# Where the low half of each weight is made: engine chosen by time to use, retention split four units ahead, down units on both sets of banks

## Chip, cores and metric

The kernel runs on one core of a Trainium2 chip. The metric is the device time of one execution in microseconds (us); the time of a kernel is the median of its runs.

## What is computed

One step of a decoder of two layers on 576 tokens (512 of a prompt, 64 of 8 samples), all in fp32. In each layer:

```python
rq, rk, rv, rg, sq, sk, sv, mq, g_ret, g_swa, g_mem = split(x @ w_in)
ret_b = (silu(rg) * group_norm(retention(rq, rk, rv, state))) @ w_br_ret
swa_b = sink_window_attend(rope(sq), rope(sk), sv, cache) @ w_br_swa
mem_b = mem_attend(mq, memory_keys, memory_values) @ w_br_mem
merged = sigmoid(g_ret) * ret_b + sigmoid(g_swa) * swa_b + sigmoid(g_mem) * mem_b
x = layer_norm(ALPHA * x + merged @ w_out)
x = layer_norm(ALPHA * x + square(relu(x @ w_up)) @ w_down)
```

For the prompt the memory keys and values are computed from 256 memory tokens (`mem_prompt @ w_mem_kv`); for the samples they come from a cache, 2 MB of keys and 2 MB of values a layer and group of four samples.

## The kernel before

**Weights.** The weights are cut into units of 128x8x128 fp32 numbers (512 KB), 154 a layer, used one after the other. To keep fp32 accuracy a unit is used as two tiles: `hi`, its value rounded to fp32r, and `lo`, what is left. A unit's matmuls go by eight slots, and each slot has three (hi by x's high part, lo by x's high part, hi by x's low part), for each of two groups of tokens, A and B, 288 columns each: 24 matmuls a unit and group. So the low part is wanted one matmul after the high part. Unit names: `mk`, `mv` (memory keys and values), `rk`, `rq`, `rv`, `rg` (retention), `sk`, `sv`, `sq` (window), `mq`; `gr`/`br`, `gs`/`bs`, `gm`/`bm` (gate and branch), `wo` (output), `up`, `ua`/`ub`, `dh`, `dn` (MLP). The MLP's middle works on pairs `ua`/`ub` in seven half-size products (`pair_steps`, `block`: their sums and casts are on VectorE and ScalarE), and between the pairs stand the half units `dh` of the down projection.

**Making the low part** (`split`, L546). A unit is loaded by SyncE's queue (`fetch`). By the first route, the DMA route, ScalarE casts (hi), ScalarE writes minus hi into lo, and a DMA issued on GpSimd's queue adds the raw unit to it. By the second (`split_into`), hi is cast on ScalarE or VectorE, whichever the planner holds free sooner (`soonest`), and VectorE subtracts. Before, the DMA route is taken by every unit from the ninth on but the second units of `dh`.

**Order.** Everything is emitted in one order, and each engine's queue keeps it. `run` goes through the steps of a stage; between the matmuls of a step `Filler` puts other work (norms, attention, retention, and `tick`, which splits the next unit) by a planner's clock (`Clock`), whose cost of each instruction is in `cost` (L320 to L329), and by each unit's due time `use`: a split is emitted when the due time is within `LOOK` = 24 us, and at most `cap` units (three) stand split and unused; within `LEAD` = 4 us it is emitted at once. Of matmul results three PSUM banks (tag "g") take the units' products, and five (tag "a") the rest. 38 buffers of 4 KB a partition (tag "T") hold raw, hi and lo tiles and the cached memory; a tile's write waits until its buffer's last reader is done. `mem_sample` loads the cached memory on GpSimd's queue: two key tiles ahead, each other tile when the one two before it has been emitted to the matmuls.

**Names.** `load_mem` loads and prepares the memory tokens of layer 1 during layer 0's `dn`; `last` of `norm_ev` is the end of a group's layer norm, which is emitted in the next stage. Names of tiles are numbered as they are made; in the rows below `T` stands for any tile of the 38.

Of the kernel before, what the change touches and what calls it, by code (L numbers as in the profile page):

```python
# [36 lines left out]
EARLY = 0.4  # L37
EARLY_PE = -0.8
LEAD = 4.0
DN_SKEW = 7  # L40
START = 3
STEP = 2
# [178 lines left out]
def mm_us(n):  # L221
    return n / 2400.0 + 0.0134
# [40 lines left out]
def dn_skew(l):  # L263
    return 8 if l == DEPTH - 1 else DN_SKEW


class Clock:
# [41 lines left out]
    @staticmethod  # L309
    def cost(eng, fn, out, ins, kw):  # L310
        n = max([out.free_size()] + [i.free_size() for i in ins])
        if eng == "tensor":
            if fn == "transpose":
                return ins[0].partition_size() / 1200.0
            n, m = out.free_size(), out.partition_size()
            if ins[0].dtype == F32R:
                return mm_us(n if n >= 256 else 4 * n)
            return 4 * n / 2400.0 * (m / 128.0 if m < 128 else 1.0)
        psum = any(i.space == PSUM for i in ins)
        if eng == "scalar":  # L320
            t = (0.05 if psum else 0.094) + n / 1200.0
            return t + 0.093 * sum(kw.get(k) is not None and not isinstance(kw[k], float)
                                   for k in ("scale", "bias", "accum_out"))
        if eng == "gpsimd":
            return 0.15 + n / 480.0
        if fn == "bn_stats" or psum or len(ins) > 1 and fn != "tensor_scalar" or fn in ("tensor_reduce", "stream_shuffle"):
            return 0.068 + n / 960.0
        return 0.065 + 0.065 * (len(ins) - 1) + n / 1920.0

    def op(self, eng, fn, out, ins, kw, store):  # L330
        te = self.te
# [117 lines left out]
class Builder:  # L449
# [96 lines left out]
    def split(self, i):  # L546
        u, k, b = self.items[i]
        if b is not None:
            self.w[i] = self.block(u, b)
            self.live[i] = 1  # L550
            return
        raw = self.raw.pop(u)
        hi = self.tile([P, 8, P], F32R)
        lo = self.tile([P, 8, P], F32R)
        if u > 7 and (k[1] != "dh" or k[2] == 0):
            self.nc.scalar.copy(hi, raw)
            self.nc.scalar.activation(lo, raw, AF.Copy, scale=-1.0)
            self.nc.gpsimd.dma_start(lo, raw, accum_op=ALU.add)
        else:
            self.split_into(hi, lo, raw, True)  # L560
        self.w[i] = (hi, lo)
        self.live[i] = 2
# [25 lines left out]
    def tick(self):  # L588
# [6 lines left out]
        u = self.items[i][0]  # L595
        urgent = self.use[i] < self.fill.t + LEAD
        if urgent or c.te["scalar"] < c.now + 0.3 and (u not in self.raw or c.ready((self.raw[u],)) < c.now):
# [36 lines left out]
            if i % 2 and i < n - 1:  # L634
                self.fill.advance(6 * mm_us(cols))

    def mstep(self, u, g, X, evac, slots=range(8)):
        n = NG[g]

        def fn():  # L640
            ps = self.bank("g")[:, :n]
            self.gemm(ps, u, list(slots), lambda i: (X[g]["h"][i // 4][:, i % 4, :], X[g]["l"][i // 4][:, i % 4, :]))
            evac(g, ps)
        return ([u], fn, 6 * mm_us(n))

    def both(self, u, X, evac, slots=range(8)):
        return [self.mstep(u, g, X, evac, slots) for g in "AB"]

    def pair_steps(self, key, XT, evac):

# [83 lines left out]
    def load_x(self, X):  # L734
# [16 lines left out]
        def split():  # L751
            for i in range(4):
# [9 lines left out]
                X[g]["l"].append(lo)  # L762
        self.between = iter(todo)
        return split()

    def load_mem(self, M):
        M["h"] = [self.tile([P, 4, 256], F32R) for _ in range(2)]
        M["l"] = [self.tile([P, 4, 256], F32R) for _ in range(2)]
        raws = [self.tile([P, 4, 256]) for _ in range(2)]
        for j in range(2):  # L770
            self.nc.scalar.dma_start(raws[j], self.I["memT"][:, 4 * j:4 * j + 4, :])
        for j in range(2):
            yield (raws[j],)
            self.split_into(M["h"][j], M["l"][j], raws[j])

    def start(self):
        M = self.M = {}
        mem = [self.tile([P, 4, 256]) for _ in range(2)]
        M["h"] = [self.tile([P, 4, 256], F32R) for _ in range(2)]
        M["l"] = [self.tile([P, 4, 256], F32R) for _ in range(2)]  # L780
# [689 lines left out]
    def layer(self, l, X):  # L1470
# [2 lines left out]
        ident = self.c("ident")  # L1473
        uid = {k: self.item[(l,) + k, None] for k in unit_order() if k[0] not in ("ua", "ub")}
        M = self.M
        mk = self.tile([P, 4, 256])
        mv = self.tile([P, 2, 512])
        mkd = self.dram([P, 4, 256])
# [3 lines left out]
        steps = []  # L1482
# [64 lines left out]
        for p in range(4):  # L1547
# [8 lines left out]
            steps = []  # L1556
# [6 lines left out]
            if p == 0 and l:  # L1563
                steps = [steps[i] for i in (0, 2, 1, 3)]
            if p == 0:
                steps = [self.lazy(s, self.before[g]) for s, g in zip(steps, "AABB" if l else "ABAB")]
# [36 lines left out]
            def rg_ev(e, sg=sg):  # L1603
                def ev(g, ps):
                    t = self.tt()[:, :NG[g]]
                    S.activation(t, ps, AF.Tanh, scale=0.5)
                    V.scalar_tensor_tensor(sg[:, e, OFF[g]:OFF[g] + NG[g]], t, 1.0, ps, ALU.add, ALU.mult)
                return ev
            for e in range(2):
                steps += self.both(uid["rg", 2 * p + e], X, rg_ev(e))  # L1610
            self.run(steps)
            self.fill.add(self.retention(l, p, qk, rv, rvs, sg, GR), 3)

        del xs
        steps = []
# [72 lines left out]
        steps = []  # L1688
# [16 lines left out]
        mq = self.pair_tiles()  # L1705
        steps = []
# [30 lines left out]
        steps = []  # L1737
# [16 lines left out]
        steps = []  # L1754
# [46 lines left out]
        steps = []  # L1801
# [8 lines left out]
        def dh(q, k, src):  # L1810
            def ev(m):
                def e(g, ps):
                    if q == 0:
                        while len(Ts) <= (m % 4) // 2 and not self.fill.idle(tg):
                            self.fill.push(tg)
                        yt = y[g][m // 4][:, m % 4, :]
                        V.scalar_tensor_tensor(yt, yt, ALPHA, ps, ALU.mult, ALU.add)
                    else:
                        yt = y[g][m // 4][:, m % 4, :]
                        V.tensor_tensor(yt, yt, ps, ALU.add)  # L1820
                return e
            r = []
            for e in range(2):
                r += self.both(uid["dh", q, k], src, ev(2 * k + e), range(4 * e, 4 * e + 4))
            return r
        self.fill.add(tg, 2)
        steps = []
# [15 lines left out]
        for q in range(2, 8):  # L1843
            H.append(self.feat_tiles(1))
            steps = []
# [10 lines left out]
            if 2 < q < 5:  # L1856
                k = ("swk", "swv")[q - 3]
# [3 lines left out]
        if True:  # L1861
            keys = [("dn", m) for m in range(8)]
            n2 = {g: self.norm_ev(g, y[g], l, 16, EPS, X2) for g in "AB"}
            if X2 is not None:
                self.M = {}
                self.fill.add(self.load_mem(self.M), 5)
            self.run(skewed(keys, H, lambda m: lambda g, ps: n2[g](m, ps), dn_skew(l), "AB" if X2 else "BA"),
                     7 if X2 else 8)
            self.before = {g: lambda g=g: n2[g].st["last"] for g in "AB"}
# [84 lines left out]
```

## Time and profile before

| | us |
|---|---|
| median of three runs | 2315.34 (2314.46 to 2324.88) |
| the profiled execution | 2317.91 |
| its span, first to last instruction | 2316.1 |
| TensorE busy | 2161.7 |
| VectorE busy | 1176.4 |
| ScalarE busy | 1023.6 |
| GpSimd busy | 236.2 |

PE is TensorE, DVE VectorE, ACT ScalarE, POOL GpSimd, SP SyncE, PEld the loading of weights into TensorE. A row of waits says which engine stood, for what, how long in total, how often, and the longest. A row of a stretch gives from:to, its length, and for each engine the busy time with the number of instructions, then the TensorE clock that was granted (1.00 is 2.4 GHz, and the half of it, 1.2 GHz, is the other level), the share of the DMA engines and GB/s. A row by form gives busy time, the mean in ns of one, and the idle time before with what ended it. A row of the timeline gives start, length, engine, operation and, in brackets, the idle time before it and what ended it. Matmuls overlap, so busy time and idle time can add up to a little more than the stretch.

### The profile page before, as it was taken

Reading aid. Unit: us, or ns where it says so; the run is one execution under the profiler, and the core shown is the slowest. Engines: PE = TensorE matmul, PEld = TensorE weight load, DVE = VectorE, ACT = ScalarE, POOL = GpSimd, SP = SyncE. Lnnn points to the kernel's source line nnn. Section 1 sums busy time; section 2 is a strip of 40 time slices with the busy share of each in tenths; the row PEclk is TensorE's granted clock in tenths of the full one; section 3 lists DMA queues with packets and bytes.
Section 4 is the critical chain, followed back from the end, with each engine's and each line's share of the span. In section 5 each row is a group of like instructions: output and inputs, shape, how many; then the busy total and the mean of one; then the engine's idle time right before and its main releaser. Section 6 shows DMA issues by size and latency. Waiting matters only on the chain. (4 is left out here: it accounts for less than half of the span.)

```text
span 2316.1 us, 39366 instructions
## 1 busy us (share of the span) xinstructions
PE 2161.7 (93%) x16180; PEld 2082.1 (90%) x16180; DVE 1176.4 (51%) x2656; ACT 1023.6 (44%) x1853; POOL 236.2 (10%) x310
## 2 busy tenths in 40 slices
PE   7999999999988999997969999999989889999987
PEld 6999999988988999997969999999889879999987
DVE  4454554134237566665734446542332465666657
ACT  4333455434456443345443333554334554443453
POOL 1111201111111000000121111011111100000000
PEclk8999999999999999998979999999999989999999
DMA  9555645667585422235684557456776744222342
GB/s 321 133 134 134 171 113 147 162 183 198 147 219 114 123 86 73 84 100 145 174 213 125 140 144 181 113 137 164 190 202 158 186 107 115 94 73 81 100 121 69
DMA packets 97269, 328.63 MB, mean 142 GB/s; under 512 B 10624, under 2 KB 20352, under 8 KB 97024
## 3 DMA queue, kind: packets, MB, share of 16 engines
q0 software_dynamic: 41056, 149.97, 30.7%
q1 hardware_dynamic: 50944, 168.27, 21.2%
q10 hardware_dynamic: 5088, 7.87, 1.1%
q8 instruction: 127, 2.08, 0.4%
q14 instruction: 54, 0.44, 0.1%
HBM read 200.89 MB, written 15.99 MB: 94 GB/s over the span
## 5 line engine op out<-in xcount | busy, mean ns | idle before, releaser
L358 PE MATMUL pg<-T,T 128*128 128x288 f32 (+1 forms) x12992 | 1816.5, 299 | 116.0 <-DMA T<-T 85.3
L358 PEld LDWEIGHTS pg<-T,T 128*128 128x128 f32 x12992 | 1763.9, 191 | 154.8 <-DMA T<-T 92.6
L358 ACT CAST T<-T 128x1024 fp32r<-128x1024 f32 (+7 forms) x502 | 391.5, 801 | 222.2 <-DVE T L358 178.7
L358 POOL DMA_DIRECT2D T<-T x212 | 183.5, 870 | 1856.5 <-ACT T L358 1574.7
L358 PE MATMUL pa<-T,T 128*128 128x288 f32 (+9 forms) x2216 | 288.9, 314 | 22.5 <-DMA T<-in_mck 11.1
L358 DVE TENSOR_TENSOR T<-T,T 128x512 fp32r<-128x512 f32 (+5 forms) x351 | 273.0, 799 | 62.8 <-ACT T L358 59.2
L358 PEld LDWEIGHTS pa<-T,T 128*128 128x128 f32 (+3 forms) x2216 | 240.0, 170 | 48.4 <-issue 22.2
L358 ACT ACTIVATE T<-T 128x1024 fp32r<-128x1024 f32 (+1 forms) x224 | 237.7, 1062 | 27.2 <-DMA T<-T 11.7
L358 ACT ACTIVATE t<-pg 128x288 f32<-128x288 f32 x128 | 52.4, 409 | 229.8 <-PE pg L358 218.3
L358 DVE TENSOR_TENSOR T<-T,pg 128x288 f32<-128x288 f32 x208 | 90.5, 451 | 100.0 <-PE pg L358 99.5
L358 DVE TENSOR_TENSOR T<-u,T 128x288 fp32r<-128x288 f32 x160 | 72.8, 455 | 122.0 <-ACT T L358 121.9
L358 ACT ACTIVATE u<-u 128x288 f32<-128x288 f32 x200 | 88.8, 444 | 90.3 <-DVE u L358 86.2
L358 DVE SCALAR_TENSOR_TENSOR T<-t,pg 128x288 f32<-128x288 f32 x64 | 29.0, 454 | 141.6 <-ACT t L358 96.8
L358 ACT CAST T<-u 128x288 fp32r<-128x288 f32 x160 | 69.2, 433 | 52.0 <-DVE u L358 47.2
L358 DVE TENSOR_TENSOR T<-T,u 128x288 f32<-128x288 f32 (+2 forms) x136 | 88.1, 660 | 3.6
L358 DVE SCALAR_TENSOR_TENSOR u<-t,pg 128x288 f32<-128x288 f32 x64 | 28.8, 451 | 101.0 <-PE pg L358 100.7
L358 ACT COPY T<-pg 128x512 f32<-128x512 f32 (+2 forms) x44 | 20.9, 478 | 121.1 <-PE pg L358 120.9
L358 ACT ACTIVATE T<-pa,rnb,rr 128x128 f32<-128x128 f32 x32 | 12.0, 456 | 118.7 <-issue 86.9
L358 DVE TENSOR_TENSOR T<-pa,T 128x512 fp32r<-128x512 f32 (+2 forms) x48 | 25.3, 535 | 64.6 <-ACT T L358 64.1
L358 DVE TENSOR_TENSOR u<-u,pa 128x288 f32<-128x288 f32 x72 | 32.7, 454 | 45.2 <-PE pa L358 45.0
L358 ACT CAST T<-pa 128x256 fp32r<-128x256 f32 (+2 forms) x36 | 15.1, 419 | 60.6 <-PE pa L358 56.4
L358 PE MATMUL pa<-cst,T 128*128 128x128 f32 (+1 forms) x306 | 40.4, 276 | 0.0
(156 smaller groups left out, 1048.9 us busy)
## 6 DMA issues: line engine op xcount, KB each, us to landing
T<-in_wall SPq DMA_DIRECT2D x305, 512.0 KB, 4.2
T<-T POOLq DMA_DIRECT2D x212, 512.0 KB, 5.5
T<-in_mck POOLq DMA_DIRECT2D x16, 512.0 KB, 6.4
T<-in_mcv POOLq DMA_DIRECT2D x16, 512.0 KB, 6.7
T<-in_s POOLq DMA_DIRECT2D x8, 512.0 KB, 8.0
out_state_s<-T POOLq DMA_DIRECT2D x8, 512.0 KB, 5.5
T<-in_xT SPq DMA_DIRECT2D x4, 576.0 KB, 10.5
T<-in_xT ACTq DMA_DIRECT2D x4, 576.0 KB, 8.0
```

What stands on the lines that cost most here:

```text
L358: r = f(*a, **kw)
```

## The change

- `split` takes the DMA route only where the due time is more than `FAR` = 11 us from the planner's time, the unit isn't of `mq`, `gs`, `bs`, `gm`, `bm`, and stands behind the sixteenth. All others go to VectorE's subtraction. Of 212 units that took the DMA route 115 keep it and 97 leave it, 70 of them with the cast on ScalarE and 27 with the cast on VectorE; in 22 second units of `dh` the cast goes from VectorE to ScalarE.
- The planner's costs of ScalarE and VectorE instructions are higher, by 0.085 to 0.11 us each.
- `run` of retention may hold four units split, not three.
- The products of `dh` for group B go to the banks "a"; group A's stay in "g".
- At the start of layer 1 all of the memory tokens' preparation that is left is emitted before anything else.

```diff
+FAR = 11.0
...
         if eng == "scalar":
-            t = (0.05 if psum else 0.094) + n / 1200.0
+            t = (0.16 if psum else 0.19) + n / 1200.0
...
         if fn == "bn_stats" or psum or len(ins) > 1 and fn != "tensor_scalar" or fn in ("tensor_reduce", "stream_shuffle"):
-            return 0.068 + n / 960.0
-        return 0.065 + 0.065 * (len(ins) - 1) + n / 1920.0
+            return 0.155 + n / 960.0
+        return 0.15 + 0.065 * (len(ins) - 1) + n / 1920.0
...
-        if u > 7 and (k[1] != "dh" or k[2] == 0):
+        if self.use[i] - self.fill.t > FAR and k[1] not in ("mq", "gs", "bs", "gm", "bm") and u > 15:
             self.nc.scalar.copy(hi, raw)
             self.nc.scalar.activation(lo, raw, AF.Copy, scale=-1.0)
             self.nc.gpsimd.dma_start(lo, raw, accum_op=ALU.add)
...
-    def mstep(self, u, g, X, evac, slots=range(8)):
+    def mstep(self, u, g, X, evac, slots=range(8), tag="g"):
...
-            ps = self.bank("g")[:, :n]
+            ps = self.bank(tag)[:, :n]
...
-    def both(self, u, X, evac, slots=range(8)):
-        return [self.mstep(u, g, X, evac, slots) for g in "AB"]
+    def both(self, u, X, evac, slots=range(8), tags="gg"):
+        return [self.mstep(u, g, X, evac, slots, tag) for g, tag in zip("AB", tags)]
...
+        if l:
+            self.fill.finish(self.memory)
...
-            self.run(steps)
+            self.run(steps, 4)
             self.fill.add(self.retention(l, p, qk, rv, rvs, sg, GR), 3)
...
-                r += self.both(uid["dh", q, k], src, ev(2 * k + e), range(4 * e, 4 * e + 4))
+                r += self.both(uid["dh", q, k], src, ev(2 * k + e), range(4 * e, 4 * e + 4), "ga")
...
-                self.fill.add(self.load_mem(self.M), 5)
+                self.memory = self.load_mem(self.M)
+                self.fill.add(self.memory, 5)
```

Three places in the order of instructions. The first is VectorE between a pair and the `dh` units behind it, before: T923 and T925 collect the down projection of groups A and B, `pg` is a bank of "g".

```order
L358 TENSOR_TENSOR T923_6639<-T923_6639,pg1281_9292 128x288
L358 TENSOR_TENSOR T1229_8895<-u1280_9287,T1228_8894 128x288
L358 CAST T1284_9317<-T1251_9059 128x1024
L358 TENSOR_TENSOR T1285_9318<-T1251_9059,T1284_9317 128x1024
L358 TENSOR_TENSOR T925_6643<-T925_6643,pg1282_9307 128x288
L358 TENSOR_TENSOR T1288_9332<-T1271_9201,T1288_9332 128x512
L358 TENSOR_TENSOR T1290_9342<-T1271_9201,T1283_9315 128x1024
L358 TENSOR_TENSOR rc1291_9343<-T1290_9342,T1271_9201 128x512
L358 TENSOR_TENSOR T1292_9346<-rc1291_9343,T1292_9346 128x512
L358 TENSOR_TENSOR T923_6639<-T923_6639,pg1289_9335 128x288
L358 TENSOR_TENSOR T925_6643<-T925_6643,pg1293_9356 128x288
```

The same place after the change.

```order
L359 TENSOR_TENSOR T923_6604<-T923_6604,pg1281_9248 128x288
L359 TENSOR_TENSOR T1227_8849<-u1279_9224,T1226_8848 128x288
L359 TENSOR_TENSOR T925_6608<-T925_6608,pa1282_9263 128x288
L359 TENSOR_TENSOR T1229_8851<-u1280_9242,T1228_8850 128x288
L359 TENSOR_TENSOR T1285_9281<-T1252_9022,T1284_9280 128x1024
L359 TENSOR_TENSOR T1289_9295<-T1273_9172,T1289_9295 128x512
L359 TENSOR_TENSOR T923_6604<-T923_6604,pg1286_9284 128x288
L359 TENSOR_TENSOR T1290_9305<-T1273_9172,T1283_9278 128x1024
L359 TENSOR_TENSOR rc1291_9306<-T1290_9305,T1273_9172 128x512
L359 TENSOR_TENSOR T1292_9309<-rc1291_9306,T1292_9309 128x512
L359 TENSOR_TENSOR T925_6608<-T925_6608,pa1293_9312 128x288
```

Group B's products are read from `pa`, the 128x1024 cast has left VectorE, and one of the reads of `pg` stands ahead of the pair's sums (128x1024, then 128x512) where it stood behind them.

The second place is GpSimd's queue while the samples' first group reads its cached memory (`in_mck` keys, `in_mcv` values), before: each `T<-T` row is the low part of a unit.

```order
L358 DMA T690_5027<-in_mck 128x1024
L358 DMA T691_5029<-in_mck 128x1024
L358 DMA T706_5107<-T674_4923 128x1024
L358 DMA T718_5200<-T686_5011 128x1024
L358 DMA T725_5272<-in_mck 128x1024
L358 DMA T726_5278<-in_mck 128x1024
L358 DMA T729_5283<-T704_5104 128x1024
L358 DMA T733_5318<-in_mcv 128x1024
L358 DMA T734_5320<-in_mcv 128x1024
L358 DMA T748_5386<-T716_5197 128x1024
L358 DMA T750_5417<-in_mcv 128x1024
L358 DMA T752_5435<-in_mcv 128x1024
```

After the change.

```order
L359 DMA T690_5010<-in_mck 128x1024
L359 DMA T691_5012<-in_mck 128x1024
L359 DMA T740_5336<-in_mck 128x1024
L359 DMA T741_5342<-in_mck 128x1024
L359 DMA T742_5352<-in_mcv 128x1024
L359 DMA T743_5354<-in_mcv 128x1024
L359 DMA T757_5456<-in_mcv 128x1024
L359 DMA T758_5466<-in_mcv 128x1024
```

The low parts have left the queue, and the eight loads follow each other. Which buffer a load takes has changed with it: by the waits in front of the instructions, T740's load waits for the last matmul on T690 (the first key tile), T741's for the last on T691, and T758's for the last on T742 (the first value tile).

The third place is VectorE at the memory projection of layer 1, after the change: T1691, T1694 and T1697 are the low parts of `mv` 1 to 3, the other rows are group B's layer norm (T925, T926).

```order
L359 SCALAR_TENSOR_TENSOR u1679_12056<-pa1667_11963,ln1678_12054 128x288
L359 TENSOR_TENSOR T925_6608<-T925_6608,pa1666_11962 128x1152
L359 TENSOR_TENSOR ln1682_12082<-ln1681_12059 128x288
L359 SCALAR_TENSOR_TENSOR ln1682_12082<-ln1682_12082,u1679_12056 128x288
L359 SCALAR_TENSOR_TENSOR u1680_12057<-ln1682_12082,ln1681_12059 128x288
L359 TENSOR_TENSOR T925_6608<-T925_6608,u1680_12057 128x576 x2
L359 TENSOR_TENSOR T926_6609<-T926_6609,pa1666_11962 128x1152
L359 TENSOR_TENSOR T926_6609<-T926_6609,u1680_12057 128x576 x2
L359 TENSOR_TENSOR T1691_12106<-T1663_11950,T1690_12105 128x1024
L359 TENSOR_TENSOR T1694_12118<-T1671_11988,T1693_12117 128x1024
```

Before, the three are made by ScalarE and GpSimd, and GpSimd's queue has them in a row.

```order
L358 DMA d30_157<-T925_6643 128x4x288
L358 DMA d30_157<-T926_6644 128x4x288
L358 DMA T1691_12178<-T1669_12062 128x1024
L358 DMA T1694_12191<-T1679_12112 128x1024
L358 DMA T1697_12204<-T1689_12175 128x1024
```

On VectorE they now stand behind the norm, with twelve more of its instructions (128x288 and 128x576) between T1694 and T1697.

## Rows read from the trace of the kernel before

**Rows 1.** The page, busy time of each engine, share of the span, instructions.
```profile
PE 2161.7 (93%) x16180; PEld 2082.1 (90%) x16180; DVE 1176.4 (51%) x2656; ACT 1023.6 (44%) x1853; POOL 236.2 (10%) x310
```

**Rows 2.** Waits of PE over the whole span: total us, times, longest.
```profile
PE pg L358 <- DMA T<-T: 85.3, 27, 8.8
PE pg L358 <- DVE T L358: 25.2, 29, 1.4
PE pa L358 <- DMA T<-in_mck: 11.1, 4, 3.9
PE pa L358 <- DMA T<-in_mcv: 10.7, 10, 2.5
```

**Rows 3.** Waits of PE in 30:60, in 75:250, in 800:1060, in 1155:1190.
```profile
PE pg L358 <- DMA T<-T: 11.8, 2, 6.5
...
PE pg L358 <- DMA T<-T: 3.4, 4, 1.4
...
PE pg L358 <- DVE T L358: 10.1, 10, 1.0
...
PE pg L358 <- DMA T<-T: 18.9, 3, 8.6
```

**Rows 4.** Stretches: length; busy (count) of PE, PEld, DVE, ACT, POOL; clock; DMA.
```profile
34.00:42.00 8.00, 5.30 (x24) 5.29 (x25) 0.00 (x0) 2.58 (x4) 1.09 (x2) 0.57 1.02 389
...
640.00:675.00 35.00, 27.68 (x184) 27.21 (x183) 10.88 (x23) 18.59 (x23) 6.88 (x8) 0.90 0.99 253
710.00:755.00 45.00, 38.66 (x266) 37.72 (x265) 26.97 (x54) 28.04 (x53) 3.44 (x4) 0.92 0.39 92
800.00:1060.00 260.00, 249.90 (x1857) 247.54 (x1856) 173.09 (x309) 105.05 (x213) 0.00 (x0) 1.00 0.26 86
1078.00:1098.00 20.00, 9.18 (x48) 8.73 (x47) 3.82 (x9) 13.77 (x20) 4.34 (x5) 0.66 0.95 237
1155.00:1192.00 37.00, 18.86 (x65) 15.57 (x66) 13.40 (x24) 17.39 (x24) 7.82 (x10) 0.68 0.68 167
1790.00:1828.00 38.00, 29.78 (x191) 29.31 (x191) 11.04 (x23) 19.37 (x24) 6.80 (x8) 0.87 0.98 256
1862.00:1908.00 46.00, 35.40 (x218) 34.38 (x217) 26.85 (x52) 26.44 (x47) 4.24 (x5) 0.85 0.42 97
2238.00:2256.00 18.00, 10.54 (x68) 10.10 (x67) 4.06 (x10) 12.98 (x19) 4.35 (x5) 0.81 0.86 192
```

**Rows 5.** Instructions by form, whole span: count, busy us, mean ns, idle before.
```profile
L358 ACT CAST T<-T 128x1024 fp32r<-128x1024 f32 x236 | 246.0, 1043 | 30.5 <-PE pg L358 23.8 <-issue 3.8 <-DMA T<-in_wall 1.3
L358 ACT ACTIVATE T<-T 128x1024 fp32r<-128x1024 f32 x212 | 223.9, 1056 | 17.9 <-DMA T<-T 11.7 <-PE pa L358 6.1
...
L358 DVE TENSOR_TENSOR T<-T,T 128x1024 fp32r<-128x1024 f32 x51 | 62.5, 1225 | 1.2 <-ACT T L358 0.3
...
L358 DVE CAST T<-T 128x1024 fp32r<-128x1024 f32 x27 | 18.6, 688 | 17.3 <-DMA T<-d 17.3
```

**Rows 6.** POOL's issues: ns min/median/max, first and last start.
```profile
L358 POOL DMA_DIRECT2D T<-T x212: 847/860/1442, 27.6 to 2262.5; - x106
```

**Rows 7.** The page, DMA issues: count, KB, median us from issue to landing.
```profile
T<-T POOLq DMA_DIRECT2D x212, 512.0 KB, 5.5
T<-in_mck POOLq DMA_DIRECT2D x16, 512.0 KB, 6.4
```

**Rows 8.** Timeline of DVE, layer norm of group B beside the memory projection.
```profile
1165.31 0.46 DVE L358 SCALAR_TENSOR_TENSOR u<-pa,ln 128x288 f32<-128x288 f32 x1 [9.85 <-PE pa L358]
...
1171.14 1.43 DVE L358 TENSOR_TENSOR T<-T,u 128x576 f32<-128x576 f32 x2
...
1177.77 0.76 DVE L358 TENSOR_TENSOR T<-T,T 128x576 fp32r<-128x576 f32 x1
```

**Rows 9.** Timeline of POOL and PE, third and fourth cached key tile, layer 0.
```profile
493.25 1.10 POOL L358 DMA_DIRECT2D T<-in_mck  x2 [1.39 <-PE pg L358]
...
499.77 1.08 PE L358 MATMUL pa<-T,T 128*32 128x256 f32 x8 [3.90 <-DMA T<-in_mck]
```

## Prediction

> **What bounds the kernel now.** First the busy times: TensorE works 93% of the span, VectorE and ScalarE about half, GpSimd a tenth [rows 1]. So the end is set by TensorE, and a change that adds no matmuls (this one doesn't) can only give back what TensorE waits, or what it does at half clock. Then the waits of TensorE [rows 2]: 85.3 us in 27 waits for `DMA T<-T`, which is the GpSimd DMA that finishes a low part; 25.2 us in 29 for VectorE; 11.1 and 10.7 us for the cached keys and values. Then the stretches around the large waits [rows 4], for the clock: around the large waits it fell to 1.2 GHz, so that the mean of the stretch is 0.57 to 0.92 instead of 1.00. A stretch's loss is its length less its matmuls at full pace, and full pace is that of 800:1060, 249.90 us for 1857 matmuls, 0.1346 us each [rows 4].
>
> **Why the low parts are late.** By the DMA route a low part takes the cast (1.043), the negation (1.056), the issue (0.86) and 5.5 us to landing: 8.5 us at the least [rows 5 to 7]. By the other route it is 1.04 or 0.69 for the cast and 1.225 for the subtraction, 2.0 to 2.3 us, if VectorE is free. The units that the planner splits late are the ones TensorE waits for. VectorE gets 97 subtractions, 97 x 1.225 = 119 us, and 5 casts more; ScalarE loses 97 negations, GpSimd 97 DMAs. So the 85.3 us are the pool that can be won, and VectorE's queue is the new place to wait.
>
> **The sum by stage**, against the profiled 2317.9 us.
>
> *Start (units 8 and 9).* 11.8 us of waits [rows 3]. In 34:42 the 24 matmuls took 5.30 us instead of 3.23, 2.1 lost by the clock; the second wait, shorter, loses about 1.6. In the new order both low parts are subtracted long before their use (36 matmuls and more). Gain 15.5; bounds 12 (the clock stays) and 15.5.
>
> *Retention.* Every odd `rg` unit waits 0.7 to 1.4 us, 3.4 in four [rows 3], and so in layer 1. With four units ahead their low parts stand over 160 matmuls ahead instead of 50. Gain 6; bounds 4 and 9, the upper one with layer 1's first `rv` unit.
>
> *Last gate unit and output projection.* Loss of 640:675: 35 - 184 x 0.1346 = 10.2; of 1790:1828: 38 - 191 x 0.1346 = 12.3 [rows 4]. Now `bm` and `wo` 1 to 4 are subtracted. `wo` 1's cast (1.04) and subtraction (1.225) stand behind the last gate's evacuation, with some 13 matmuls (1.75) to cover them, so 0.5 to 2.5 of wait stay; I take 1.5 a layer, since other ScalarE work stands ahead. Gain 22.5 - 3 = 19.5; bounds 14 and 21.
>
> *Up.* Loss of 710:755: 45 - 266 x 0.1346 = 9.2; of 1862:1908: 46 - 218 x 0.1346 = 16.7 [rows 4]. Here the subtraction meets an obstacle: in the new order `up` 6's low part stands on VectorE behind group B's norm, and `up` 7's behind the norm's last scaling. The norm's chain takes from 1165.31 to 1171.14 + 1.43 = 1172.6, 7.3 us, and the scaling lasts to 1177.77 + 0.76 = 1178.5, 6.0 us more [rows 8]. `up` 6 is used 44 matmuls (5.9 us) after the chain starts: 7.3 + 0.45 + 1.225 - 5.9 = 3.1 of wait. `up` 7 comes 24 matmuls (3.2) later: 6.0 + 0.8 + 1.225 - 3.2 = 4.8. With half a microsecond at group A's norm and some 3 lost by the clock that is 11.4 a layer, 22.8 of the old 25.9. Gain 3; bounds -5 (both waits a half longer) and 14 (the chain is done early).
>
> *Pairs.* TensorE waits 1.01 us once in each of 20 periods (10.1 in 10 in layer 0, [rows 3]): the third `dh` product needs a bank of "g", whose reader on VectorE stands behind the pair's sums. With group B in "a" the three "g" banks last twice as long and that reader moves ahead of the sums. Gain 20.2; bounds 14 (a third replaced by the subtraction just ahead of it) and 24 (with the other waits on VectorE).
>
> *Down, first unit.* Loss of 1078:1098: 20 - 48 x 0.1346 = 13.5; of 2238:2256: 18 - 68 x 0.1346 = 8.8 [rows 4]. Now VectorE does the low part: two operations of 128x288 (0.46 each, as in [rows 8]), cast 0.69, subtraction 1.225, 2.8 us, against 13 matmuls (1.75). 1.1 stays in each layer. Gain 20.1; bounds 15 and 22.
>
> *Memory projection of layer 1.* 18.9 us of waits [rows 3], and in 1155:1192 the mean clock is 0.68 [rows 4], 11.8 us of full clock missing; TensorE worked in about half of the stretch, so I count half, 5.9. Now `mk` 3 is early. But `mv` 1's subtraction stands behind group B's norm: 7.3 + 1.2 = 8.5 us from the norm's start, against 5.1 us of matmuls (18 and 13 of two wider forms): 3.5. `mv` 3's stands behind the scaling, another 3.0, and the clock takes perhaps 3. Gain 24.8 - 9.5 = 15.3; bounds 8 and 22.
>
> *Cached memory.* This is a loss. GpSimd's queue no longer carries the low parts here, but the loads take other buffers: the third key tile's load waits for the last matmul on the first one, and its own matmuls come four matmuls later. Before, it was issued at 493.25 and TensorE waited 3.9 us until 499.77 [rows 9]. Now nearly all of 6.4 us to landing [rows 7] is on the path, about 6; the fourth value tile, issued after the first one's use, costs about 5.5 more. The second group gets its tiles early, and about 2 stay there, for its softmax between two products. Old waits, both layers: 11.1 + 10.7 = 21.8 [rows 2]; new: 2 x (6 + 5.5 + 2) = 27. Loss 5; bounds a loss of 16 (landings of 9 us) and a gain of 3 (landings of 4.8).
>
> *VectorE elsewhere.* 97 subtractions of 1.225 us, each able to hold up the reading of a bank. Today the 51 subtractions of this form waited 1.2 us in all, and TensorE's waits on VectorE other than the pairs' come to 5 us [rows 2, 5]. Most banks have 25 matmuls (3.4 us) for an evacuation of two operations of 0.46, so one subtraction ahead fits and two don't. I take 5, bounds 0 and 24 (a fifth of 119).
>
> *Costs and the memory's preparation emitted at once:* they only set the order, which is counted above; nothing more.
>
> Sum: 15.5 + 6 + 19.5 + 3 + 20.2 + 20.1 + 15.3 - 5 - 5 = 89.6. 2317.9 - 89.6 = 2228.3; the profiled run stands 2.6 above the median, so 2225.7, rounded to **2225**.
>
> **A rule beside the rows.** The 212 issues of these DMAs on GpSimd took 847 to 1442 ns, the median 860, beside all that VectorE did [rows 6], so no issue was held up by more than 0.6 us. The Trainium skill, page "SBUF — State Buffer", section "SBUF: two separate sides", says that an fp32 copy within SBUF on VectorE locks GpSimd out, so that a DMA issued there waits until VectorE is done; that speaks against moving work to VectorE. By that rule each of eight cached tiles that TensorE stands for could come one cast (0.69, [rows 5]) later, 5.5 us, and the time would be 2231. The trace doesn't agree as far as these issues show it.
>
> **The rivals.**
> 1. *The subtractions cost TensorE half their length.* VectorE runs its queue in order; where a subtraction waits for a cast or stands ahead of a bank's reader, TensorE stops. At half of 1.225 for each of 97 that is 59 us, not 5: 2225 + 54 = 2279. For it: the obstacle is real at `up` and `mv`, and VectorE is busy 27 of 45 and of 46 us there [rows 4]. Against it: among the pairs, where it is busiest, no unit moves, and in the other stages it is half idle.
> 2. *Slower than before.* The same place with the full price: in the gate and output stages every moved subtraction delays the readers of all three "g" banks, so that TensorE waits for its whole length, and the half clock follows. 97 x 1.225 = 119 instead of 5: 2225 + 114 = 2339. It decides from about 1.1 us for each moved unit. Against it: VectorE is busy 11 of 35 and 11 of 38 us in these stages [rows 4], and ScalarE, which makes the cast, loses more work than VectorE gets.
> 3. *The page's rule above*: 2231.
>
> That the change doesn't do what it says is excluded: the order shows the moved units.
>
> **How the numbers follow.** The forecast (my sum, its terms within their bounds) 0.78, rival 1 0.10, rival 2 0.03, the rule 0.05, and 0.04 for a mixture of the first two that ends near today's time. Terms' bounds that all fall one way give 2185 and 2290, which isn't likely; with the largest (cached memory, VectorE elsewhere, up, memory projection, each 7 to 20 us to a side) combined as independent, 22 us to either side hold the forecast's time 8 times in 10. The range is wider, down to 2188 since all losses are guesses of mine that may be too dark, and up to 2270 towards rival 1: that leaves out rivals 1 and 2, the mixture, and a little of the forecast. A measurement of this kernel can tell about 0.5% from no change, 2304 to 2327. Faster than that: forecast, rival 1 and the rule, 0.93; within: 0.04; slower: 0.03.
>
> **What would show it.** In the changed trace: waits of TensorE for `DMA T<-T` near zero; waits on VectorE of 3 to 5 us at `up` 6 and 7, and 3 us at `mv` 1 and 3; no 1.01 us per pair; at the third cached key tile and the fourth value tile of each layer's first group 5 to 6 us each; VectorE's busy time up by about 120 us, ScalarE's and GpSimd's down by about 100 and 84. Many new waits of TensorE for VectorE below 1 us would be rival 1. The prediction is wrong if waits for `DMA T<-T` come back at units that keep the DMA route, or if weights land late because retention holds more buffers.

## The result

The changed kernel takes 2205.65 us (2205.05 to 2207.34), the kernel before, run beside it, 2318.03 (2314.46 to 2324.88): a ratio of 0.951, interval 0.949 to 0.954. That is faster, as forecast, inside the range of 2188 to 2270 and 19.4 us below the 2225 predicted. The profiled execution took 2205.09 us, its span 2203.2.

The page of the changed kernel, the row that answers [rows 1]:

```profile
PE 2131.3 (97%) x16180; PEld 2066.1 (94%) x16180; DVE 1285.2 (58%) x2752; ACT 929.2 (42%) x1757; POOL 151.0 (7%) x213
```

TensorE does the same 16180 matmuls in 30.4 us less, in the main since its clock fell less often (mean granted clock 0.983, 0.971 before). VectorE's busy time is up by 109 us, ScalarE's down by 94, GpSimd's by 85. The waits of TensorE over the whole span, which answer [rows 2]:

```profile
PE pg L359 <- DVE T L359: 21.6, 15, 4.1
PE pg L359 <- ACT T L359: 11.1, 4, 7.5
PE pa L359 <- DMA T<-in_mck: 7.9, 4, 3.8
PE pa L359 <- DMA T<-in_mcv: 7.9, 4, 3.8
PE pa L359 <- ACT T L359: 2.5, 3, 1.0
PE pa L359 <- DVE T L359: 2.5, 7, 0.4
PE pa L359 <- ACT u L359: 2.0, 2, 1.0
```

The row that led before, 85.3 us for `DMA T<-T`, is gone: there is no such wait left. Rows for VectorE are now 15 waits and not 29, but longer ones, and a new one for ScalarE stands second, with 7.5 us in one piece. The stretches, in the form of [rows 4]: last gate and output, `up` 6 and 7, the pairs, the first down unit, the memory projection:

```profile
620.00:660.00 40.00, 37.77 (x270) 37.32 (x269) 25.21 (x46) 18.02 (x25) 2.57 (x3) 0.96 0.63 176
690.00:725.00 35.00, 29.14 (x189) 28.68 (x188) 21.93 (x37) 20.76 (x42) 0.00 (x0) 0.85 0.07 25
750.00:1005.00 255.00, 255.00 (x1914) 255.00 (x1914) 174.10 (x311) 116.98 (x224) 0.00 (x0) 1.00 0.26 91
1015.00:1045.00 30.00, 27.80 (x201) 26.75 (x200) 20.53 (x36) 20.41 (x39) 0.92 (x1) 1.00 0.52 186
1085.00:1130.00 45.00, 32.47 (x189) 28.83 (x189) 36.14 (x59) 22.71 (x40) 3.48 (x5) 0.85 0.52 167
```

The pairs run without a gap: 255.00 us busy of 255.00, at 255.00 / 1914 = 0.1332 us a matmul. `up` and the memory projection still fall to 1.2 GHz for a part (mean clock 0.85). The landings, in answer to [rows 7], and below them GpSimd's issues, in answer to [rows 6]:

```profile
T<-T POOLq DMA_DIRECT2D x115, 512.0 KB, 5.5
T<-in_mck POOLq DMA_DIRECT2D x16, 512.0 KB, 4.4
T<-in_mcv POOLq DMA_DIRECT2D x16, 512.0 KB, 5.1
```

```profile
L359 POOL DMA_DIRECT2D T<-T x115: 832/850/924, 66.9 to 2146.3; - x115
L359 POOL DMA_DIRECT2D T<-in_mck x16: 527/530/531, 449.2 to 1641.3; - x16
```

A low part takes the same 5.5 us, but a cached key tile lands in 4.4 and not 6.4, a value tile in 5.1 and not 6.7.

Set against each other by the start of the first matmul of the same unit in both profiled runs, the gains by stage are:

| stage | predicted (bounds) | measured |
|---|---|---|
| start | 15.5 (12 to 15.5) | 15.4 |
| retention | 6 (4 to 9) | 10.9 |
| last gate, output | 19.5 (14 to 21) | 16.5 |
| up | 3 (-5 to 14) | 7.1 (-0.9 in layer 0, 8.0 in layer 1) |
| pairs | 20.2 (14 to 24) | 28.2 |
| down, first unit | 20.1 (15 to 22) | 18.7 |
| memory projection | 15.3 (8 to 22) | 9.7 |
| cached memory | -5 (-16 to 3) | 6.3 |
| VectorE elsewhere | -5 (-24 to 0) | 0 (no remainder) |
| sum | 89.6 | 112.8 |

### The profile page after: what moved, and what is told of

It reads as the page before. It is cut to its first block, busy times and chain, and to the rows that moved or that the text cites. A ratio compares the mean times of both kernels' runs of the same rounds, so it can differ in the third digit from the quotient of the medians.

```text
span 2203.2 us, 39044 instructions
## 1 busy us (share of the span) xinstructions
PE 2131.3 (97%) x16180; PEld 2066.1 (94%) x16180; DVE 1285.2 (58%) x2752; ACT 929.2 (42%) x1757; POOL 151.0 (7%) x213
## 4 chain that ended last, share of the span: by engine, by line
PE 85%; issue 6%; DVE 5%; DMA 2%; ACT 1%; SPq 0%; POOL 0%; DVEq 0%; POOLq 0%; ACTq 0%
PE pg L359 63%; PE pa L359 22%; DVE T L359 4%; DMA T<-in_wall 1%; ACT T L359 1%; DMA T<-in_mck 1%; ACT u L359 1%; DMA T<-in_mcv 0%; DMA T<-T 0%; DVE u L359 0%; DVE ln L359 0%; SPq L359 0%; DVE accB L359 0%; DVE rc L359 0%; DVE s L359 0%
## 5 line engine op out<-in xcount | busy, mean ns | idle before, releaser
L359 PE MATMUL pg<-T,T 128*128 128x288 f32 (+1 forms) x11840 | 1648.9, 297 | 33.0 <-DVE T L359 21.6
L359 PEld LDWEIGHTS pg<-T,T 128*128 128x128 f32 x11840 | 1599.5, 190 | 56.9 <-DVE T L359 25.6
L359 PE MATMUL pa<-T,T 128*128 128x288 f32 (+8 forms) x3368 | 456.8, 308 | 20.9 <-DMA T<-in_mck 7.9
L359 PEld LDWEIGHTS pa<-T,T 128*128 128x128 f32 (+3 forms) x3368 | 400.0, 176 | 47.2 <-DMA T<-in_mck 10.7
L359 DVE TENSOR_TENSOR T<-T,T 128x1024 fp32r<-128x1024 f32 (+7 forms) x448 | 389.8, 889 | 85.7 <-ACT T L359 75.0
L359 POOL DMA_DIRECT2D T<-T x115 | 98.7, 858 | 1485.1 <-ACT T L359 1092.1
L359 ACT ACTIVATE T<-T 128x1024 fp32r<-128x1024 f32 (+1 forms) x127 | 135.5, 1067 | 14.9 <-DVE T L359 10.8
L359 DVE TENSOR_TENSOR T<-T,pg 128x288 f32<-128x288 f32 x128 | 57.5, 449 | 38.4 <-PE pg L359 38.0
L359 DVE TENSOR_TENSOR T<-T,pa 128x288 f32<-128x288 f32 (+1 forms) x92 | 52.2, 568 | 17.7 <-PE pa L359 15.5
L359 ACT CAST T<-pa 128x512 fp32r<-128x512 f32 (+2 forms) x40 | 17.3, 438 | 52.9 <-PE pa L359 48.9
```

Source lines behind the costliest of these rows:

```text
L359: r = f(*a, **kw)
```

## The experiments

Each is the changed kernel with the edit shown, and all are compared with the kernel before on the same chip (2318 to 2321 us). The time of the changed kernel, 2205.7, is the mark for the edits.

**What each part carries.** First the old condition for the DMA route, with all else as changed.

```diff
-        if self.use[i] - self.fill.t > FAR and k[1] not in (...) and u > 15:
+        if u > 7 and (k[1] != "dh" or k[2] == 0):
```

> The changed kernel with one part undone: all units from the ninth on but the second units of dh take the DMA route again (212 low parts by DMA instead of 115). Theory A, that the gain is the shorter way of late low parts (2.0 to 2.3 us on VectorE instead of 8.5 us): TensorE's waits for the low-part DMA come back, some 75 us in about 25 waits at units 8 and 9, wo, up, dn 0 and the memory projection, with their half clock; 2285 us, and only the pairs' 25 us stay. Theory B, that the planner's higher costs made the gain by another order: the waits stay below 20 us and the time below 2230.

Measured 2299.3 (2296.1 to 2306.1), ratio 0.992 [0.990, 0.995]: 94 us of the gain go with this one condition. The waits came back as theory A has them; the time is 14 us longer than it said. Its waits of TensorE, and two landings from its page:

```profile
PE pg L359 <- DMA T<-T: 74.9, 19, 8.9
PE pa L359 <- DMA T<-in_swk: 13.6, 2, 7.3
PE pa L359 <- DMA T<-in_mcv: 10.2, 10, 2.4
```

```profile
T<-in_mck POOLq DMA_DIRECT2D x16, 512.0 KB, 6.9
T<-in_mcv POOLq DMA_DIRECT2D x16, 512.0 KB, 7.8
```

The low parts are late again, and the cached tiles land even later than in the kernel before (6.9 and 7.8 us, 6.4 and 6.7 there). In retention, with four units ahead, the odd `rg` units don't wait any more, but the first `rv` units do: this row is 55:260, layer 0's retention, and in layer 1 there is one wait of 1.4.

```profile
PE pg L359 <- DMA T<-T: 3.9, 2, 2.8
```

Set against the kernel before by the same units, layer 0's retention gains 0.1 us here, where the changed kernel gains 4.4.

Next, group B's `dh` products go back to the banks "g":

```diff
-                r += self.both(uid["dh", q, k], src, ev(2 * k + e), range(4 * e, 4 * e + 4), "ga")
+                r += self.both(uid["dh", q, k], src, ev(2 * k + e), range(4 * e, 4 * e + 4))
```

> The changed kernel with group B of the dh units back in the banks g. Theory A: TensorE waits again once in each of 20 periods, 1.01 us each and 0.26 more to get going again, and the waits between the first dh units come back too: 28 us, 2233 us, periods of 25.27 instead of 24.00 us. Rival: part of the periods' gain came from the higher planner costs and the casts moved to ScalarE; then the period is below 24.7 us and the time below 2222.

Measured 2229.6 (2228.0 to 2230.7), 0.962 [0.960, 0.964]: the banks give 24 us. Two neighbouring stalls of TensorE among its pairs, from the timeline:

```profile
818.25 8.26 PE L359 MATMUL pg<-T,T 128*128 128x288 f32 x60 [0.81 <-DVE T L359]
...
843.32 2.93 PE L359 MATMUL pg<-T,T 128*128 128x288 f32 x20 [0.81 <-DVE T L359]
```

They stand 25.07 us apart with 180 matmuls between, and 180 matmuls take 24.00 without a stall. So a recorded wait of 0.81 costs 1.07. In the kernel before it was 1.01 recorded and a period of 25.27, 1.27 lost:

```profile
823.29 8.26 PE L358 MATMUL pg<-T,T 128*128 128x288 f32 x60 [1.01 <-DVE T L358]
...
848.56 0.66 PE L358 MATMUL pg<-T,T 128*128 128x288 f32 x3 [1.01 <-DVE T L358]
```

The 0.26 on top was the same in both. Theory A is right but for 0.2 us of each stall, which the rest of the change took away.

Next, the planner's old costs:

```diff
-            t = (0.16 if psum else 0.19) + n / 1200.0
+            t = (0.05 if psum else 0.094) + n / 1200.0
...
-            return 0.155 + n / 960.0
-        return 0.15 + 0.065 * (len(ins) - 1) + n / 1920.0
+            return 0.068 + n / 960.0
+        return 0.065 + 0.065 * (len(ins) - 1) + n / 1920.0
```

> The changed kernel with the planner's old costs of ScalarE and VectorE. Theory A: the costs matter only where they set the order. The memory tokens of layer 1 are cast well ahead of the layer again, so that the 7.5 and 0.8 us at its first matmuls go, with some 3 us of half clock; the low parts of up 6 and 7 are split earlier, 2 to 10 us less; the cached tiles of the first group come as late as now. 2195 us. Theory B, that the higher costs are what brings the low parts early: 20 us or more are lost, above 2225.

Measured 2180.7 (2178.4 to 2182.5), 0.941 [0.939, 0.943]: without this part of the change the kernel is 25 us faster. Theory B fell; theory A has the way but not the size, and one of its points failed: the wait for the memory tokens' casts stays, 5.4 us instead of 7.5 (the last row). By stage, in the profiled runs, `up` gives 10.6 us, the last gate and output 5.6, cached memory 4.0, the memory projection 2.6. Waits of TensorE, and then VectorE and TensorE at layer 0's `up` 6:

```profile
PE pg L359 <- DVE T L359: 12.0, 12, 3.5
PE pa L359 <- DMA T<-in_mcv: 9.0, 5, 3.9
PE pa L359 <- DMA T<-in_mck: 8.3, 4, 4.0
PE pg L359 <- ACT T L359: 6.3, 3, 5.4
```

```profile
687.59 0.46 DVE L359 SCALAR_TENSOR_TENSOR u<-pa,ln 128x288 f32<-128x288 f32 x1
```

```profile
696.78 3.46 PE L359 MATMUL pg<-T,T 128*128 128x288 f32 x24 [0.97 <-DVE T L359]
```

The same place in the changed kernel, VectorE's norm chain and the low part behind it, and TensorE (this answers [rows 8]):

```profile
698.17 0.46 DVE L359 SCALAR_TENSOR_TENSOR u<-pa,ln 128x288 f32<-128x288 f32 x1 [1.25 <-ACT ln L359]
...
705.72 1.22 DVE L359 TENSOR_TENSOR T<-T,T 128x1024 fp32r<-128x1024 f32 x1
```

```profile
706.99 5.68 PE L359 MATMUL pg<-T,T 128*128 128x288 f32 x24 [3.77 <-DVE T L359]
714.76 7.50 PE L359 MATMUL pg<-T,T 128*128 128x288 f32 x43 [2.09 <-DVE T L359]
```

TensorE comes to `up` 6 at 706.99 - 3.77 = 703.2, 5.0 us after the chain's start; with the old costs at 695.8, 8.2 us after it. The chain itself is as long as ever. So at `up` the costs act by the order: with the higher ones a norm stands later against the matmuls. They also move work, as the planner's costs decide which engine is held free sooner. The casts of hi on VectorE, in the changed kernel and then with the old costs:

```profile
L359 DVE CAST T<-T 128x1024 fp32r<-128x1024 f32 x32 | 22.0, 686 | 0.1
```

```profile
L359 DVE CAST T<-T 128x1024 fp32r<-128x1024 f32 x61 | 41.9, 687 | 0.0
```

29 casts go from ScalarE (1.05 us each) to VectorE (0.69). No run tells what of the 25 us is due to them and what to the order.

Last, three units ahead in retention and not four:

```diff
-            self.run(steps, 4)
+            self.run(steps, 3)
```

> The changed kernel with retention's limit back to three units split ahead. Theory A: with fewer units ahead fewer are due in more than 11 us, so more of them (13) go to VectorE, whose 2.3 us fit; the waits of 0.7 us at the odd rg units do not come back in full. 2206 to 2212 us. Rival, that the limit is what removed retention's waits: 11 us slower, 2217, with the waits of 0.7 us at the odd rg units.

Measured 2206.1 (2204.8 to 2209.5): no difference, as theory A has it; of waits in retention there is one, of 1.1 in layer 1. Only 102 low parts go by DMA now instead of 115, so units that are split later fall under `FAR` and go to VectorE by themselves.

Then the route alone: old costs, both groups' `dh` products in the banks "g", three units ahead, in one kernel (the three diffs above together).

> The changed kernel with the old planner costs, three units ahead in retention and group B's dh products back in the banks g: of the change only the new choice of route is left (and the memory tokens' preparation emitted at the start of layer 1). Theory A (the terms add up: with the old costs alone 2180.7, banks gg alone cost 23.9, cap three costs nothing): 2180.7 + 23.9 = 2205, so the choice of route alone would carry 113 us of the whole, and banks and costs nearly cancel. Theory B (the parts lean on each other, the route needs the higher costs or the second set of banks): 2225 or more, with new waits of TensorE for T<-T or for VectorE at the pairs above 45 us in all.

Measured 2213.7 (2210.5 to 2216.3), 0.955 [0.953, 0.957]. So the choice of route carries some 105 us by itself, as theory A has it, and the banks' gain and the costs' loss nearly cancel. The sum misses by 9. In the profiled runs 6.4 of it lie at the pairs, whose wait is 1.01 again and not 0.81 (20 x 0.2 = 4), with more lost ahead of the first pair; 1.1 in the memory projection, where `mv` 3 has a wait of 2.4 that the run with old costs doesn't have; most of the rest where the cached memory is used (the waits for `in_mck`, `in_mcv` and `in_swk` are 20.4 together, 17.9 with the old costs alone).

**Why the route helps: late low parts, or a crowded queue?** The list of unit names is dropped, so that units of `mq`, `gs`, `bs`, `gm` and `bm` that have time take the DMA route:

```diff
-        if self.use[i] - self.fill.t > FAR and k[1] not in ("mq", "gs", "bs", "gm", "bm") and u > 15:
+        if self.use[i] - self.fill.t > FAR and u > 15:
```

> The changed kernel without the list of unit names: the units mq, gs, bs, gm and bm take the DMA route when they are due in more than 11 us, 52 low parts more by DMA. Theory A: these units are early, so their low parts don't wait by either route, but the cached tiles share the queue and the DMA engines with them again: landings of 6 us or more instead of 4.4 to 5.1, and 3 to 10 us more in the waits for cached tiles; 2205 to 2215 us. Rival, that the gain in these stages comes from relief of the DMA route itself: waits for the low-part DMA come back and the time is above 2225.

Measured 2236.7 (2232.8 to 2247.0), 0.965 [0.963, 0.968]: 31 us slower for 52 more DMAs. Neither theory held: the landings are as long as A has them, but the time is the rival's, and almost none of it is at the low parts themselves (1.5 us):

```profile
PE pa L359 <- DVE T L359: 11.8, 9, 4.7
...
PE pa L359 <- DMA T<-in_mcv: 10.5, 10, 2.9
PE pa L359 <- DMA T<-in_swk: 10.4, 2, 7.1
```

```profile
388.51 0.85 POOL L359 DMA_DIRECT2D T<-T  x1 [5.33 <-ACT T L359]
393.59 0.56 POOL L359 DMA_DIRECT2D T<-in_swk  x1 [4.23 <-DMA T<-T]
```

```profile
398.65 2.09 PE L359 MATMUL pa<-T,u 64*32 64x128 f32 x64 [3.33 <-DMA T<-in_swk]
```

```profile
480.03 1.29 DVE L359 TENSOR_TENSOR T<-pa,T 128x512 fp32r<-128x512 f32 x2 [6.66 <-DMA T<-T]
```

```profile
T<-in_mck POOLq DMA_DIRECT2D x16, 512.0 KB, 7.0
T<-in_mcv POOLq DMA_DIRECT2D x16, 512.0 KB, 7.8
```

A low part on its way does harm in two ways here. The load of the window's cached keys (`in_swk`), behind it on GpSimd's queue, waits 4.23 us until such a DMA has landed, and TensorE 3.33 for the keys. VectorE's write of a tile waits 6.66 us for another one, with TensorE behind it. Both wait for a landing and not for a turn in the queue; by the buffer rule above that is a tile which such a DMA still uses, though the rows don't name the buffer. The cached tiles land in 7.0 and 7.8 us instead of 4.4 and 5.1, but TensorE's recorded waits for them did not grow: 12.7 us in all, against 15.8 in the changed kernel.

The kernel before, with 212 such DMAs, has neither harm: no row for `in_swk`, and for VectorE's tiles in "a" only this one.

```profile
PE pa L358 <- DVE T L358: 0.7, 2, 0.3
```

By stage this run is 15 us slower than the kernel before around the window and 9 in cached memory. So what the list of names saves is in the main a loss that comes with the rest of the change, and not a part of the 113 us; against the kernel before, the cached-memory stage gains the 6.3 of the table. What in the new order brings these two waits no run shows.

**The waits that are left.** The third cached tile in the changed kernel, on GpSimd and on TensorE, answers [rows 9]:

```profile
481.25 1.05 POOL L359 DMA_DIRECT2D T<-in_mck  x2 [30.37 <-PE pa L359]
```

```profile
485.18 1.08 PE L359 MATMUL pa<-T,T 128*32 128x256 f32 x8 [3.82 <-DMA T<-in_mck]
```

It is issued when the first tile's last matmul is done, and TensorE stands for all of the landing but a little. The third tile's matmuls of keys and of values are given later places:

```diff
         for b in range(4):
+            if b == 2:
+                yield 5.0
             yield Pe((kt[b], qz))
...
         for b in range(4):
+            if b == 2:
+                yield 5.0
             yield Pe((vt[b], pz))
```

> The changed kernel with one edit: the planner puts 5 us of other work ahead of the third cached key tile and the third cached value tile of each group, so that other matmuls stand between a load and its use (47 matmuls or more instead of 4). Theory A, that the waits of 3.8 and 3.8 us in each layer are the loads' own time after their buffer came free, with nothing between load and use: they fall below 1 us each; 15 us of waits and some 5 of half clock, 2187 us. Rival: what stands between is taken from elsewhere and the same time is waited later, above 2200.

Measured 2189.5 (2187.2 to 2190.9): 16 us less, the waits for cached tiles gone, as theory A has it. Then `up` 6 and 7 are made urgent 12 us ahead of use:

```diff
-        urgent = self.use[i] < self.fill.t + LEAD
+        urgent = self.use[i] < self.fill.t + (12.0 if self.items[i][1][1:] in (("up", 6), ("up", 7)) else LEAD)
```

> The changed kernel with one edit: the splits of up 6 and 7 are urgent 12 us ahead of use instead of 4, so that their subtractions stand ahead of group B's norm on VectorE. Theory A, that these two waits (3.8 and 2.1 us in layer 0, 4.1 and 1.7 in layer 1) are the norm's chain of 7 us ahead of the subtraction: they go, with 3 to 5 us of half clock in each layer; 2188 us. Rival: the norm itself is delayed by the two subtractions, and the first units that use its result wait 2.5 us in each layer; gain below 8 us.

Measured 2192.6 (2190.1 to 2193.9): 13 us less, as theory A has it; the waits for VectorE's tiles fall from 21.6 to 13.2. Then the memory tokens, for which the longest wait of all stands. In the changed kernel, ScalarE and TensorE at the start of layer 1:

```profile
1093.18 2.17 ACT L359 ACTIVATE T<-T,par 128x288 fp32r<-128x288 f32 x4
1095.25 2.92 ACT L359 CAST T<-T 128x1024 fp32r<-128x1024 f32 x3
```

```profile
1096.33 0.80 PE L359 MATMUL pg<-T,T 128*128 128x256 f32 x2 [7.48 <-ACT T L359]
```

The casts of the memory tokens stand behind group A's norm, though the tokens were loaded by about 1045. They are put on a lane that doesn't wait for idle engines:

```diff
-                self.fill.add(self.memory, 5)
+                self.fill.add(self.memory, 4)
```

> The changed kernel with one edit: the preparation of layer 1's memory tokens no longer waits until the planner sees both ScalarE and VectorE idle, but goes as soon as the tokens are loaded. Theory A, that the 7.5 us wait at the first matmuls of the memory projection is this cast, 50 us after the tokens landed, forced at the start of the layer behind the norm of group A: that wait and the 0.8 behind it go, with about 3 us of half clock; 2195 us. Rival, that the projection waits for the norm or its banks anyway: under 3 us gained, the wait reappears at the same place with another name.

Measured 2207.1 (2206.6 to 2207.8): nothing gained; theory A fell, the rival holds. The 7.5 us are gone, and VectorE's norm and subtractions stand in their place:

```profile
1102.46 2.72 PE L359 MATMUL pg<-T,T 128*128 128x256 f32 x11 [4.16 <-DVE T L359]
```

Four shorter waits of 0.8 to 2.1 us follow, and the stage is as long as before within 0.2 us.

**Together.** Old costs with the held-back cached products:

> The changed kernel with the old planner costs and with the two cached-memory products of each group given 5 us more of the planner's time. Theory A (the waits for cached tiles and the planner's costs are separate): with old costs TensorE still waits 17.3 us for in_mck and in_mcv; most of that and the half clock behind it go, as the same edit took 16.1 us off the changed kernel: 2180.7 - 16 = 2165. Rival (the products that are held back run into retention's end and the gate units, so the wait only moves): 2175 to 2180, with new waits of 2 to 4 us for ScalarE or VectorE between the cached products and the first gate.

Measured 2161.3 (2159.9 to 2162.3), 0.932 [0.930, 0.934]; the edits add up (19 us here, 16 above). With `up` 6 and 7 urgent earlier as well:

> As the run with old costs and held-back cached products, and up 6 and up 7 are split 12 us ahead of use, not 4. Theory A: in layer 0 the wait of about 1 us at up 6 goes, in layer 1 (3.5 us) little changes because the order has the subtraction no earlier: 2160 to 2163. Rival: the earlier subtractions hold up group A's norm, 2165 or above.

Measured 2161.5 (2161.0 to 2164.8): no difference. The wait of 0.97 at `up` 6 goes, and the waits for a cached key tile and for `in_swk` grow by about half a microsecond each, to 1.3 and 1.1. And with the memory tokens' lane on top:

> As the run with old costs, held-back cached products and up split 12 us ahead, and the memory tokens of layer 1 are prepared on a lane that is not held for idle time. Theory A (with the old costs the tokens are cast in time by themselves): same as without it within 3 us, 2158 to 2165. Rival (the 5.4 us wait for ScalarE at the memory projection goes and nothing takes its place): 2152 to 2156.

Measured **2156.4** (2155.1 to 2160.0), 0.930 [0.928, 0.933], the fastest of all, 49 us below the changed kernel. The time lies between the two theories. Here moving the memory tokens' casts is worth about 5 us, 3.8 of them at the memory projection by the profiled runs, where alone it was worth nothing. The wait of 5.4 for ScalarE is gone, but VectorE takes part of its place there, with a longest wait of 4.4:

```profile
PE pg L359 <- DVE T L359: 14.3, 12, 4.4
...
PE pa L359 <- DVE T L359: 2.1, 6, 0.4
PE pg L359 <- DMA T<-T: 1.3, 2, 1.1
```

TensorE's mean clock is 0.994 there (0.983 in the changed kernel, 0.971 before).

## Why the prediction was right, and where its terms were off

**The mechanism held.** The waits for low parts were the pool, the subtractions fitted, and the only long waits on VectorE are the ones named, at `up` 6 and 7 and `mv` 1 (3.4 us; 3.5 predicted). The long wait for ScalarE was not named. That the route carries it is shown by the two runs with the route undone and with the route alone.

**The sum is nearer than its terms.** Against the measured stages the terms are too low by 33 us and too high by 10, so a part of the miss cancels. And the planner's costs, put at nothing, take 25 us: with the old ones the time is 2180.7, below the range.

**Start and first down unit** came out within 1.5 us. **Last gate and output**: 16.5 and not 19.5, since the waits that stay are 1.4 for the cast and 0.9 for the subtraction, 2.2 a layer instead of 1.5, with a short fall of the clock behind them. Both waits come with the higher costs: with the old ones they are absent (one of 1.3 for a low part comes in layer 1) and the stage gains 5.6 more.

**Retention**: 10.9, above the upper bound. The cause was wrong, too: I gave the gain to the fourth unit ahead. The route alone, with three units ahead and the old costs, leaves no wait in retention; with the new costs it leaves one of 1.1 in layer 1. The fourth unit with the old route removes those at the odd `rg` units, but leaves 3.9 us in layer 0 and 1.4 in layer 1 at the first `rv` units. The size was off by the price of a stall: layer 0 gave 4.4 for four recorded waits of 3.4 in all, 0.25 more for each; layer 1 gave 6.5, with the wait at its first `rv` unit, which I had counted only in the bound.

**Pairs**: 28.2, above the upper bound of 24. The term that was mis-sized is the price of one stall. I took the recorded wait, 1.01; the period shrank by 25.27 - 24.00 = 1.27, as TensorE's step after a stall is slow as well. That is 25.4 in 20. The rest is 2.5 a layer from waits of the same kind (the longest 1.4) ahead of the first pair, less 1.1 for a new wait of 1.0 for a cast behind the last. My full pace of 0.1346 us a matmul held this loss too: its stretch has ten of the stalls, and 24.00 us for 180 matmuls is 0.1333.

**Up**: 7.1 and not 3. The waits are 3.77 at `up` 6 (3.1 predicted) and 2.09 at `up` 7 (4.8). The second was too dark: I let `up` 7 come 24 full-pace matmuls later, but the first wait drops the clock, the 24 take 5.68 us and not 3.2, and meanwhile VectorE gets ahead. A wait at half clock hides part of the next one.

**Memory projection**: 9.7 and not 15.3. The failed step is "now `mk` 3 is early": I didn't look at what `mk` 0 needs besides its weights. The memory tokens' casts wait for group A's norm, a new wait of 7.5. "Costs and the memory's preparation emitted at once: nothing more" was wrong with it, and wrong for the costs altogether, which lose 25 us. All runs of the changed kernel emit the preparation at the start of layer 1, so whether that, or the work moved between the engines, left the casts so late is not shown. The costs were counted in the order, at `up` and `mv`, but I didn't ask what the same stages would be without them. And `mv` 3's wait is 0.8, not 3.0, probably as the clock had fallen and `mv` 1's wait came first.

**Cached memory**: a gain of 6.3, where I had a loss of 5 and a bound of 3. The failed step is the landing: I took the median 6.4 from a trace in which low parts share the queue and the DMA engines with these loads. With them gone the waits are 3.8 and 2.8 to 3.8 instead of 6 and 5.5. My own bound of 4.8 for the landing was near; I chose the other end though the change itself removed what made it long. The 2 us in the second group did come, about 2 a layer, as waits for ScalarE (the 1.0 each of `ACT u`) and VectorE.

**VectorE elsewhere**: the stages above make up the whole gain, so nothing is left for it, where I took 5; the small new waits for VectorE (2.5 us at `pa` instead of 0.7) lie in the stages. Its queue had the room that the stretches of the gate stages showed. This also settles the first two rivals: at half the subtractions' length the time would have been 2279, at the whole 2339.

**The rule beside the rows.** GpSimd's issues became shorter and more even, 832 to 924 ns for the low parts (847 to 1442 before) and 527 to 531 for the cached keys, with 97 more fp32 operations on VectorE. But these rows don't test the rule as I took them to. The Trainium skill, page "SBUF — State Buffer", section "SBUF: two separate sides", says that an fp32 copy within SBUF on VectorE locks GpSimd out; of the operations that moved to VectorE 97 are subtractions of two inputs, and only 5 are casts. In neither profiled run does an issue of a low part or of a cached tile fall beside a 128x1024 cast on VectorE. And the longest issue before, 1442 ns at 1180.1, ran while VectorE was idle. What is shown is that the cached tiles came sooner and not later, against rival 3.

## What to carry to other kernels

When several engines can make an operand, choose by the time until its use: the long way through a DMA only where all of its latency is covered, the short way elsewhere. A DMA taken off a shared queue can pay twice, at its own consumer and at the loads that shared queue, buffers and engines with it, so a landing time from the crowded trace can be too long for the new one (here 6.4 us against 4.4). Measure the parts of a bundled change alone: here one (the planner's costs) took back as much as another (the banks) gave.

## What was not expected of the hardware

A stall of TensorE of about 1 us among the pairs, at full clock, costs 0.26 us more than its recorded wait: the matmul after it is followed by a step of 0.24 us instead of 0.13, and the rest, 0.16, lies in the pipelined end that the record counts as busy (shown by periods of 25.27 and 25.07 against 24.00 with waits of 1.01 and 0.81).

A cached tile of 512 KB on GpSimd's queue lands in 4.0 to 5.6 us (medians of keys and values in the eleven kernels that keep the queue free for it), and in 6.4 to 7.8 in the three where low parts' DMAs stand between the loads (before, the old condition, no list of names). The low parts' own landing is 5.4 to 5.7 in all fourteen.
